# Rotary low-order score product over all 128 rows, and a last projection in four groups of 512 columns

## The chip, the cores and the metric

The kernel runs on one core of one Trainium2 chip, as one launch. The metric is the device time of a run in microseconds (us): 1482.35 us is the median of three runs of the kernel before (1480.5 to 1486.15). The core's engines are named as the profile names them: PE is TensorE (PEld is its loading of weights), DVE is VectorE, ACT is ScalarE, POOL is GpSimd, SP is SyncE, which issues the DMAs.

## What is computed

Two layers of a mixer over 256 context rows and 256 latent rows of width 2048. Each layer normalises and modulates its rows, multiplies by one input projection, and feeds two branches: multi-head latent attention (8 heads, 128 plain and 64 rotary dimensions in a head) and a long convolution of 1024 channels. Both are normalised, gated, joined to 2048 channels and multiplied by one output projection. The second layer computes its queries and its output for the latent rows alone.

The two places that the change touches, in the reference:

```python
s = jnp.einsum("bqhd,bkhd->bhqk", q_nope, k_nope, preferred_element_type=F32)
s = s + jnp.einsum("bqhr,bkr->bhqk", q_rope, k_rope, preferred_element_type=F32)
p = jax.nn.softmax(s * SCALE, axis=-1)
...
y = jnp.concatenate([rmsnorm(o_mla, lp["grp_g_mla"]) * g_m,
                     rmsnorm(y_h, lp["grp_g_hy"]) * g_h], axis=-1)
return rmsnorm(y @ lp["w_out"], lp["post_g"])      # then x + g_x * (...)
```

## The kernel before

**Split products.** Nearly every matrix product takes its fp32 operands as a sum of two parts, a rounded high part (`hi`) and the rest (`lo`), and adds three products: hi·hi, hi·lo, lo·hi (`mm3`). Each of the three is one matmul with its own weight load. Inside a matmul call the first tensor is the one that is loaded (128 columns of it), the second the one that streams through (256 or 512 columns).

**Rotary scores.** In `head_job` the scores of one head and 128 queries are one PSUM tile (`mis` in the profile) made by five matmuls: three of `mm3` over the 128 plain dimensions, and two over the rotary ones. A rotary part has only 64 rows, so `pair_job` stacks its two parts over 128 partitions: for the even head of a pair, rows 0 to 63 hold `hi` and rows 64 to 127 hold `lo`; for the odd head the other way round. The rotary key is written twice over, in both halves, as `kr.hi` and `kr.lo` (`kr_evac` copies it to the second half before the split). One matmul over all 128 rows against `kr.hi` gives (hi + lo)·key-hi. The fifth, line 1191, takes the 64 rows `rr` that hold the query's `hi` against `kr.lo` and gives hi·key-lo.

In layer 0 a head has four such tiles: two against 512 keys and two against 256. In layer 1 it has two, against 512. With 8 heads that is 32 fifth matmuls in layer 0, half of them 512 columns wide and half 256, and 16 in layer 1 of 512 columns.

**The last output projection.** Layer 1's output has 256 rows and 2048 columns over a depth of 2048. `w_items` with `rows=True` makes it in column groups: in one group the gated rows `ys` are loaded (128 of depth by 128 output rows, `m` = 0 or 1), and the weights stream. A group of 256 columns is cut into four items of 512 KB; an item holds four depth tiles (`j`) of 256 columns. So there are 8 groups of 4 items, and each item is 4 x 2 x 3 = 24 matmuls. Each item is loaded by DMA, split into hi and lo on ACT and DVE, and then used. At the end of a group `out_evac` takes the two PSUM tiles (`acc`): ACT squares each and sums the squares into `oss`, DVE multiplies each by the gate. For the last four items, `by_rows` has PE do all of `m` = 0 first and then all of `m` = 1, and `finish` runs for each `m` on its own: sum of squares, `rs` on POOL, four multiply-adds on DVE, four stores.

**What sets the order.** Every operation is issued by a list scheduler (`Net.run`) that keeps an estimated clock of each engine. Its price of a PE operation counts the streamed columns: it doesn't look at the number of rows. Items of the weight stream ("products", rank 10) fill PE between the steps of the attention heads and the convolution. The order that results is fixed at build time.

Of the kernel before, what the change touches and what calls it, by code (L numbers as in the profile page):

```python
# [9 lines left out]
F32 = mybir.dt.float32  # L10
F32R = mybir.dt.float32r
AF = mybir.ActivationFunctionType
ALU = mybir.AluOpType
# [156 lines left out]
class Net:  # L170
# [16 lines left out]

# [1 line left out]
    # Jobs yield operations. A list scheduler issues, of those that could start first by an  # L189
    # estimate of every engine's queue, the one of the lowest rank, so that no queue is held up  # L190
    # by an operation that waits while another one could run.
    def start_of(self, op):
# [120 lines left out]

# [1 line left out]
    def job(self, name, gen, after=(), want=8, rank=5):  # L315
# [109 lines left out]

# [1 line left out]
    def split(self, hi, lo, src):  # L427
# [70 lines left out]

# [1 line left out]
    def setup(self):  # L500
# [67 lines left out]

# [1 line left out]
    def ada_first(self, sec, t0, t1):  # L570
# [121 lines left out]

# [1 line left out]
    def sine(self, n, ps, b, freq):  # L694
# [99 lines left out]

# [1 line left out]
    def load_x(self):  # L796
# [64 lines left out]

# [1 line left out]
    def w_items(self, src, width, xs, evac, need=(), rows=False, parts=False):  # L863
        hold = {}
        out = []
        dup = width == 64
        wid = P if dup else width
        mt = wid // P
        for b in range(4):
            def load(raws, b=b):  # L870
                if dup:
                    yield self.dma(raws[0][:, 512:768], src[b])
                else:
                    yield from self.load(raws[0], src[b])

            def prep(raws, hi, lo):
                if dup:
                    v = raws[0][:, 512:768].rearrange("p (j c) -> p j c", j=4)
                    h = hi[:, 0:512].rearrange("p (j r c) -> p j r c", j=4, r=2)
                    yield from self.split(h[:, :, 0], h[:, :, 1], v)  # L880
                elif isinstance(raws[0], Pair):
                    for k in range(2):
                        r = slice(k * 512, (k + 1) * 512)
                        yield from self.split(hi[:, r], lo[:, r], raws[0].halves[k])
                else:
                    yield from self.split(hi, lo, raws[0])

            def pe(w, b=b, ms=range(mt), js=range(4)):
                if parts or "ps" not in hold:
                    if len(self.acc.free) < mt:  # L890
                        yield lambda: len(self.acc.free) >= mt
                    hold["ps"] = [self.acc.get() for _ in range(mt)]
                for j in js:
                    x = xs(4 * b + j)
                    first, last = ((b == 0 or parts) and j == js[0]), ((b == 3 or parts) and j == js[-1])
                    n = free_size(x.hi)
                    for m in ms:
                        ps = hold["ps"][m]
                        if rows:
                            yield from self.mm3(ps[:, 0:wid], x[:, m * P:(m + 1) * P], w[:, j * wid:(j + 1) * wid],  # L900
                                                first, last)
                        elif dup:
                            both = w.hi[:, j * P:(j + 1) * P]
                            yield self.mm(ps[:, 0:n], both, x.hi, first, False)
                            yield self.mm(ps[:, 0:n], both, x.lo, False, last)
                        else:
                            yield from self.mm3(ps[:, 0:n], w[:, j * wid + m * P:j * wid + (m + 1) * P], x,
                                                first, last)

            def post(b=b, ms=range(mt)):  # L910
                ps = list(hold["ps"])
                for m in ms:
                    if parts and m not in hold:
                        hold[m] = (yield from self.sget())[0]
                        yield self.either(hold[m], ps[m])
                    elif parts:
                        yield self.tt(hold[m], hold[m], ps[m], ALU.add)
                    else:
                        yield from evac(m, ps[m])
                    self.acc.put(ps[m])  # L920
                if parts and b == 3:
                    for m in range(mt):
                        yield from evac(m, hold[m])
                        self.slots.put(hold[m])
            out.append(Item(load, prep, pe, post if b == 3 or parts else None,
                            need=need(b) if callable(need) else (need if b == 0 else ()), halves=not dup))
        return out
# [104 lines left out]

# [1 line left out]
    def raw_evac(self, l, tile0, name, parts, width, c0, n):  # L1034
# [59 lines left out]

# [1 line left out]
    def pair_job(self, l, hp, nq):  # L1096
# [76 lines left out]
    def head_job(self, l, h, nq):  # L1173
# [3 lines left out]
        kk, qq = st["qk"].pop(h)  # L1177
        rr = slice(i * ROPE, (i + 1) * ROPE)
        rq, kr = res["r"][i], st["kr"]
# [3 lines left out]
        for q0, nk in (((nq - L, T),) if nq == L else ((L, T), (0, L))):  # L1183
            pr = []
            pps = []
            for qi in range(2):
                r = slice(q0 + qi * P, q0 + (qi + 1) * P)
                (ps,) = yield from self.pget()
                yield from self.mm3(ps[:, 0:nk], qq[:, r], kk[:, 0:nk], True, False)
                yield self.mm(ps[:, 0:nk], rq[:, r], kr.hi[:, 0:nk], False, False)  # L1190
                yield self.mm(ps[:, 0:nk], rq[rr, r], kr.lo[rr, 0:nk], False, True)
                (p,) = yield from self.sget()
                sm = self.small.tile([P, 4], F32, tag="sm", name="sm")
                yield self.vmax(sm[:, 0:1], ps[:, 0:nk])
                yield self.ts(sm[:, 1:2], sm[:, 0:1], -SCALE, None, ALU.mult)
                yield self.act(p[:, 0:nk], ps[:, 0:nk], AF.Exp, bias=sm[:, 1:2], scale=SCALE, accum_out=sm[:, 2:3])
                self.mis.put(ps)
                yield self.recip(sm[:, 3:4], sm[:, 2:3])
                yield self.either(p[:, 0:nk], p[:, 0:nk], sm[:, 3:4])
                pr.append(p)  # L1200
# [50 lines left out]

# [1 line left out]
    def conv(self, l, ps, ci, nq):  # L1253
# [176 lines left out]

# [1 line left out]
    def z_evac(self, s, g):  # L1432
# [70 lines left out]

# [1 line left out]
    def out_evac(self, g):  # L1505
        st = self.st[1]

        def evac(m, ps):
            if g == 0 and m == 0:
                st["oss"] = self.const.tile([P, 2, 8], F32, name="oss")  # L1510
                st["zo"] = []
                for _ in range(2):
                    st["zo"].append((yield from self.sget(4)))
            j, o = divmod(g * 256, 512)
            junk = (yield from self.sget())[0]
            yield self.act(junk[:, 0:256], ps[:, 0:256], AF.Square, accum_out=st["oss"][:, m, g:g + 1])
            self.slots.put(junk)
            yield self.tt(st["zo"][m][j][:, o:o + 256], ps[:, 0:256], self.gate[j][:, o:o + 256], ALU.mult)
        return evac
# [24 lines left out]

# [1 line left out]
    def layer_items(self, l, nq):  # L1546
# [76 lines left out]
    def build(self):  # L1623
# [52 lines left out]
        for s in (1, 0):  # L1676
            for g in range(8):
                r = slice(s * L, (s + 1) * L)
                need = (lambda b: tuple(f"ys0_{4 * b + j}" for j in range(4))) \
                    if (s, g) == (1, 0) else ()  # L1680
                items += self.w_items(a["p_wout"][0, g], 256, lambda kt, r=r: self.st[0]["ys"][kt][:, r],
                                      self.z_evac(s, g), need)
# [22 lines left out]
        def need_y(b):  # L1705
            return tuple(f"ys1_{4 * b + j}" for j in range(4)) + ("gate",)
        for g in range(8):
            items += self.w_items(a["p_wout"][1, g], 256, lambda kt: self.st[1]["ys"][kt],
                                  self.out_evac(g), need_y if g == 0 else (), rows=True)
# [62 lines left out]
def lay_out(i):  # L1772
# [30 lines left out]
    def tiles(v):  # L1803
        n = v.shape[-1] // 256
        return v.reshape(2, 4, 4, P, n, 256).transpose(0, 4, 1, 3, 2, 5).reshape(2, n, 4, P, 1024)
    o["p_win"] = np.concatenate([tiles(w[:, :, 0:OFF_KR]), tiles(w[:, :, OFF_HY:OFF_GH]),
                                 tiles(w[:, :, OFF_GM:OFF_HY]), tiles(w[:, :, OFF_GH:])], axis=1)
    o["p_wkr"] = w[:, :, OFF_KR:OFF_GM].reshape(2, 4, 4, P, 64).transpose(0, 1, 3, 2, 4).reshape(2, 4, P, 256)
    o["p_wout"] = tiles(i["w_out"])
    uq = i["w_uq"].reshape(2, 4, P, HEADS, HEAD_Q)  # L1810
# [25 lines left out]
```

## Time and profile before

| | before |
|---|---|
| runs | 1480.5, 1482.35, 1486.15 us |
| the profiled execution, first to last instruction | 1483.1 us |
| PE busy | 1457.0 us, 98% |
| DVE busy | 1190.2 us, 80% |
| ACT busy | 692.6 us, 47% |
| DMA queue q1, share of 16 engines | 64.6% |

The profile gives one execution. Its time is its span: no separate time of that execution outside the span is shown. A PE matmul's duration overlaps with that of the next one, so a rate is read from starts: the start of one merged row to the start of the next, divided by the matmuls in the first. By the trace the kernel's stages lie so: up to about 316 us the modulation, the filters and layer 0's first products; 316 to 548 layer 0's attention heads, with weight items between them; 548 to 800 the convolution and the rest of layer 0's input products; 800 to 1158 layer 0's output projection, the step between the layers and layer 1's first products; 1158 to 1278 layer 1's heads; 1278 to 1382.9 the rest of its input products; 1382.9 to 1475.2 the last projection; then the tail.

### The profile page before, as it was taken

The numbers are of one execution on the slowest core, as the hardware profiler recorded it, in microseconds if no ns is written. First come the engines' busy times: TensorE is split into PE (matmuls) and PEld (weight loads), VectorE is DVE, ScalarE is ACT, GpSimd is POOL, SyncE is SP. The second block draws the span as 40 slices with busy tenths as digits, with TensorE's granted clock in tenths as the row PEclk, the third lists the DMA queues.
The fourth block names the chain that finished last, engine by engine and source line by source line (L and its number), as shares of the span: only waits on it lengthen the run. The fifth ranks groups of instructions, "written<-read, shape, count | busy, mean of one in ns | idle before, by whom it ended". The sixth has DMA issues, their size and how long they took to land.

```text
span 1483.1 us, 26318 instructions
## 1 busy us (share of the span) xinstructions
PE 1457.0 (98%) x9700; PEld 1261.2 (85%) x9700; DVE 1190.2 (80%) x2522; ACT 692.6 (47%) x1339; POOL 16.4 (1%) x20
## 2 busy tenths in 40 slices
PE   7999999999999999999999999999999999999997
PEld 5677787778787777877778999999999989999997
DVE  5577999997888878998888988888868878786544
ACT  5421354335354452334334444566646666655542
POOL 0000000000000000000000000000000000000000
PEclk9999999999999999999999999999999999999999
DMA  9997875468466677566858886567728234668441
GB/s 324 356 334 239 286 263 205 159 212 308 151 195 215 223 250 251 170 228 220 299 191 301 296 281 196 167 227 260 245 89 310 90 113 133 234 201 288 164 143 57
DMA packets 165872, 328.92 MB, mean 222 GB/s; under 512 B 18501, under 2 KB 41068, under 8 KB 165744
## 3 DMA queue, kind: packets, MB, share of 16 engines
q1 hardware_dynamic: 165744, 327.25, 64.6%
q8 instruction: 76, 1.25, 0.3%
q14 instruction: 52, 0.43, 0.1%
HBM read 301.99 MB, written 25.18 MB: 221 GB/s over the span
## 4 chain that ended last, share of the span: by engine, by line
PE 88%; DMA 7%; DVE 2%; issue 1%; SPq 1%; ACT 1%; POOL 0%; DVEq 0%; POOLq 0%; ACTq 0%
PE acc L232 68%; PE mis L232 17%; PE mis L235 3%; DMA s<-in_p_ada_first 1%; DMA raw<-in_p_ada_first 1%; DMA s<-in_p_ada_slow 1%; DVE s L250 1%; DMA s<-in_p_win 1%; SPq L309 1%; DMA s<-in_ctx 1%; DVE junk L280 1%; DMA s<-in_p_uv 0%; DMA raw<-in_p_win 0%; DMA s<-in_p_ada_rest 0%; DMA h_d<-s 0%
## 5 line engine op out<-in xcount | busy, mean ns | idle before, releaser
L232 PE MATMUL acc<-s,hi 128*128 128x256 f32 (+1 forms) x2304 | 566.0, 337 | 0.5 <-ACT hi L243 0.4
L232 PE MATMUL acc<-s,s 128*128 128x256 f32 (+1 forms) x3216 | 489.4, 308 | 0.0
L232 PEld LDWEIGHTS acc<-s,s 128*128 128x128 f32 x3216 | 439.2, 191 | 30.5 <-issue 3.7
L232 PEld LDWEIGHTS acc<-s,hi 128*128 128x128 f32 x2304 | 388.4, 191 | 56.2 <-issue 11.5
L250 DVE TENSOR_TENSOR s<-s,s 128x512 fp32r<-128x512 f32 (+5 forms) x575 | 342.2, 623 | 42.3 <-ACT s L245 21.2
L232 PE MATMUL acc<-s,raw 128*128 128x256 f32 (+1 forms) x1104 | 371.1, 336 | 0.3 <-DVE raw L250 0.3
L280 DVE SCALAR_TENSOR_TENSOR junk<-s,s 128x512 bf16<-128x512 f32 x352 | 241.5, 686 | 26.9 <-DMA s<-crow_d 10.5
L232 PE MATMUL mis<-s,s 128*128 128x256 f32 (+2 forms) x1232 | 251.4, 341 | 1.2 <-ACT s L243 0.9
L232 PEld LDWEIGHTS acc<-s,raw 128*128 128x128 f32 x1104 | 210.3, 191 | 23.0 <-issue 2.5
L232 PEld LDWEIGHTS mis<-s,s 128*128 128x128 f32 (+1 forms) x1232 | 190.4, 189 | 43.9 <-issue 13.9
L243 ACT CAST s<-s 128x512 fp32r<-128x512 f32 (+3 forms) x324 | 180.3, 589 | 74.8 <-DVE s L250 28.5
L243 ACT CAST hi<-raw 128x1024 fp32r<-128x1024 f32 (+1 forms) x100 | 97.2, 972 | 121.4 <-PE acc L232 68.7
L250 DVE TENSOR_TENSOR raw<-raw,hi 128x1024 fp32r<-128x1024 f32 x88 | 107.3, 1220 | 19.7 <-ACT hi L243 19.1
L243 ACT CAST hi<-s 128x512 fp32r<-128x512 f32 x124 | 73.4, 618 | 92.9 <-PE acc L232 75.6
L250 DVE TENSOR_TENSOR raw<-s,hi 128x512 fp32r<-128x512 f32 x124 | 83.8, 686 | 34.4 <-ACT hi L243 33.4
L243 ACT COPY s<-mis 128x512 f32<-128x512 f32 (+3 forms) x101 | 48.6, 485 | 116.7 <-PE mis L232 90.5
L250 DVE TENSOR_TENSOR s<-mis,s 128x512 fp32r<-128x512 f32 (+2 forms) x128 | 84.6, 669 | 22.8 <-ACT s L243 17.3
L243 ACT CAST s<-mis 128x512 fp32r<-128x512 f32 (+1 forms) x100 | 56.6, 570 | 89.2 <-PE mis L235 48.3
L245 ACT ACTIVATE s<-acc 128x256 f32<-128x256 f32 (+1 forms) x88 | 37.5, 429 | 96.6 <-PE acc L232 81.2
L235 PE MATMUL mis<-ident,s 128*128 128x128 f32 (+1 forms) x369 | 66.8, 291 | 4.1 <-DMA s<-in_x 1.0
L250 DVE TENSOR_TENSOR s<-raw,s 128x512 fp32r<-128x512 f32 x106 | 69.8, 683 | 0.8 <-ACT s L243 0.7
L243 ACT CAST s<-raw 128x512 fp32r<-128x512 f32 x106 | 61.8, 617 | 9.1 <-DMA raw<-in_p_wout 6.2
(85 smaller groups left out, 916.9 us busy)
## 6 DMA issues: line engine op xcount, KB each, us to landing
s<-in_p_ada_slow SPq DMA_DIRECT2D x208, 256.0 KB, 3.3
raw<-in_p_win SPq DMA_DIRECT2D x99, 512.0 KB, 5.1
s<-in_p_win SPq DMA_DIRECT2D x178, 256.0 KB, 5.3
s<-in_p_wout SPq DMA_DIRECT2D x108, 256.0 KB, 4.9
raw<-in_p_wout SPq DMA_DIRECT2D x42, 512.0 KB, 3.8
s<-in_p_ada_first SPq DMA_DIRECT2D x62, 256.0 KB, 5.8
raw<-in_p_ada_first SPq DMA_DIRECT2D x25, 512.0 KB, 6.1
raw<-in_p_ada_rest SPq DMA_DIRECT2D x20, 512.0 KB, 4.7
```

The lines of the kernel that those rows point to most:

```text
L232: lambda: self.nc.tensor.matmul(out, lhsT, rhs, start=start, stop=stop), 0.2)
L235: return Op("pe", 0.11, [out], [in_], lambda: self.nc.tensor.transpose(out, in_, ident), 0.2)
L243: self.nc.scalar.copy(out, in_)
L245: self.nc.scalar.activation(out, in_, func, **kw)
L250: return Op("dve", fixed + n * rate, [out], ins, lambda: getattr(self.nc.vector, name)(out=out, **kw))
L280: lambda: self.nc.vector.scalar_tensor_tensor(out=junk, in0=a, scalar=1.0, in1=b, op0=ALU.mult, op1=ALU.mult, accum_out=acc))
L309: return Op("sp", n / 360e3, [dst], [src], lambda: self.nc.sync.dma_start(dst, src))
```

## The change

One matmul in five of the rotary scores now runs over all 128 rows, as the one before it does. It then also adds lo·key-lo. The last projection runs over four groups of 512 columns; an item is still 512 KB, but holds two depth tiles of 512 columns, so a group has eight items and an item 2 x 2 x 3 = 12 matmuls. The weights of the last projection are laid out for that on the host and are an input of their own. The evacuation of a group works on 512 columns. The diff, without removed comments:

```diff
@@ w_items
-        mt = wid // P
-        for b in range(4):
+        mt = 2 if rows else wid // P
+        nj = 1024 // width if rows else 4
+        nb = KT // nj
+        for b in range(nb):
...
-            def pe(w, b=b, ms=range(mt), js=range(4)):
+            def pe(w, b=b, ms=range(mt), js=range(nj)):
...
-                    x = xs(4 * b + j)
-                    first, last = ((b == 0 or parts) and j == js[0]), ((b == 3 or parts) and j == js[-1])
+                    x = xs(nj * b + j)
+                    first, last = ((b == 0 or parts) and j == js[0]), ((b == nb - 1 or parts) and j == js[-1])
@@ head_job
-        rr = slice(i * ROPE, (i + 1) * ROPE)
...
-                yield self.mm(ps[:, 0:nk], rq[rr, r], kr.lo[rr, 0:nk], False, True)
+                yield self.mm(ps[:, 0:nk], rq[:, r], kr.lo[:, 0:nk], False, True)
@@ out_evac
-                st["oss"] = self.const.tile([P, 2, 8], F32, name="oss")
+                st["oss"] = self.const.tile([P, 2, 4], F32, name="oss")
...
-            j, o = divmod(g * 256, 512)
-            yield self.act(junk[:, 0:256], ps[:, 0:256], AF.Square, accum_out=st["oss"][:, m, g:g + 1])
+            yield self.act(junk, ps, AF.Square, accum_out=st["oss"][:, m, g:g + 1])
-            yield self.tt(st["zo"][m][j][:, o:o + 256], ps[:, 0:256], self.gate[j][:, o:o + 256], ALU.mult)
+            yield self.tt(st["zo"][m][g], ps, self.gate[g], ALU.mult)
@@ build
-            return tuple(f"ys1_{4 * b + j}" for j in range(4)) + ("gate",)
-        for g in range(8):
-            items += self.w_items(a["p_wout"][1, g], 256, lambda kt: self.st[1]["ys"][kt],
+            return (f"ys1_{2 * b}", f"ys1_{2 * b + 1}", "gate")
+        for g in range(4):
+            items += self.w_items(a["p_wout1"][g], 512, lambda kt: self.st[1]["ys"][kt],
                                   self.out_evac(g), need_y if g == 0 else (), rows=True)
@@ lay_out
-    o["p_wout"] = tiles(i["w_out"])
+    o["p_wout0"] = tiles(i["w_out"][0:1])[0]
+    o["p_wout1"] = i["w_out"][1].reshape(8, 2, P, 4, 512).transpose(3, 0, 2, 1, 4).reshape(4, 8, P, 1024)
```

On every engine the order of instructions is the same up to the last projection; the heads' matmuls stand where they stood (the order names a matmul by its output, so a row does not tell how many rows it multiplies). The first difference on PE is the first item of the last projection. Names there: `acc_181` and `acc_182` are the PSUM tiles of output rows 0 to 127 and 128 to 255, the first name behind the arrow is the streamed weight (hi or lo), the second the loaded `ys`. Before:

```order
L232 MATMUL acc_181_16036<-s_2039_15891,s_1980_15493 128x256
L232 MATMUL acc_181_16036<-s_2041_15893,s_1980_15493 128x256
L232 MATMUL acc_181_16036<-s_2039_15891,s_1980_15493 128x256
L232 MATMUL acc_182_16037<-s_2039_15891,s_1980_15493 128x256
L232 MATMUL acc_182_16037<-s_2041_15893,s_1980_15493 128x256
L232 MATMUL acc_182_16037<-s_2039_15891,s_1980_15493 128x256
L232 MATMUL acc_181_16036<-s_2039_15891,s_1981_15500 128x256
L232 MATMUL acc_181_16036<-s_2041_15893,s_1981_15500 128x256
```

And now:

```order
L232 MATMUL acc_181_16036<-s_2039_15891,s_1980_15493 128x512
L232 MATMUL acc_181_16036<-s_2041_15893,s_1980_15493 128x512
L232 MATMUL acc_181_16036<-s_2039_15891,s_1980_15493 128x512
L232 MATMUL acc_182_16037<-s_2039_15891,s_1980_15493 128x512
L232 MATMUL acc_182_16037<-s_2041_15893,s_1980_15493 128x512
L232 MATMUL acc_182_16037<-s_2039_15891,s_1980_15493 128x512
L232 MATMUL acc_181_16036<-s_2040_15892,s_1981_15500 128x512
L232 MATMUL acc_181_16036<-s_2042_15894,s_1981_15500 128x512
```

The sequence of three by two stays; each matmul is twice as wide, and the next depth tile (`s_1981`) comes with the next half of the weights, so that an item is over after two depth tiles. The other place is the end of DVE's queue: the last multiply by the gate, the sum for `rs`, and the four multiply-adds of output rows 128 to 255. One piece of the difference:

```order
-L250 TENSOR_TENSOR s_2087_16212<-acc_196_17062,s_1988_15544 128x256
+L250 TENSOR_TENSOR s_2101_16254<-acc_188_16616,s_1988_15544 128x512
 L289 TENSOR_REDUCE mf<-oss 128x1
 L250 TENSOR_SCALAR ms<-mf 128x1
-L250 SCALAR_TENSOR_TENSOR s_2084_16209<-s_2084_16209,rf,s_1993_15559 128x512
-L250 SCALAR_TENSOR_TENSOR s_2085_16210<-s_2085_16210,rf,s_1994_15560 128x512
-L250 SCALAR_TENSOR_TENSOR s_2086_16211<-s_2086_16211,rf,s_1995_15561 128x512
```

The same steps follow each other there; only the multiply by the gate, and ACT's square before it, have 512 columns.

## Rows read from the trace of the kernel before

**Rows 1.** The page: busy us, share of the span and instructions of each engine

```profile
PE 1457.0 (98%) x9700; PEld 1261.2 (85%) x9700; DVE 1190.2 (80%) x2522; ACT 692.6 (47%) x1339; POOL 16.4 (1%) x20
```

**Rows 2.** Windows: length, busy PE, PEld, DVE, ACT, POOL (instructions), granted clock, DMA share, GB/s

```profile
316.00:548.00 232.00, 231.66 (x1145) 180.10 (x1144) 194.31 (x485) 112.58 (x215) 0.00 (x0) 1.00 0.66 216
548.00:800.00 252.00, 251.33 (x1163) 198.40 (x1162) 222.46 (x460) 88.35 (x139) 2.77 (x2) 1.00 0.69 237
1158.00:1278.00 120.00, 119.15 (x830) 105.39 (x829) 96.35 (x203) 74.86 (x156) 0.00 (x0) 1.00 0.39 127
1382.90:1475.20 92.30, 92.28 (x769) 92.07 (x768) 46.72 (x84) 38.87 (x93) 0.55 (x1) 1.00 0.33 112
```

**Rows 3.** PE's waits, 174.8 to 1475 us: total, times, longest; first and last of five

```profile
PE mis L232 <- ACT s L243: 0.9, 1, 0.9
...
PE mis L232 <- DVE s L250: 0.2, 1, 0.2
```

**Rows 4.** Groups by form on PE: count, busy us, mean ns

```profile
L232 PE MATMUL mis<-s,s 128*128 128x512 f32 x544 | 145.6, 398 | 0.1
L232 PE MATMUL mis<-s,s 128*128 128x256 f32 x640 | 91.8, 285 | 1.1 <-ACT s L243 0.9 <-DVE s L250 0.2
...
L232 PE MATMUL mis<-s,s 64*128 64x512 f32 x32 | 15.9, 495 | 0.0
...
L232 PE MATMUL mis<-s,s 64*128 64x256 f32 x16 | 6.1, 380 | 0.0
```

**Rows 5.** Timeline of PE, a score tile of 512 keys: start, us, instructions

```profile
322.92 1.50 PE L232 MATMUL mis<-s,s 128*128 128x512 f32 x5
324.35 0.50 PE L232 MATMUL acc<-s,hi 128*128 128x512 f32 x1
324.68 0.39 PE L232 MATMUL acc<-s,raw 128*128 128x512 f32 x1
```

**Rows 6.** Timeline of PE, a score tile of 256 keys

```profile
502.05 0.94 PE L232 MATMUL mis<-s,s 128*128 128x256 f32 x5
502.92 0.50 PE L232 MATMUL acc<-s,hi 128*128 128x512 f32 x1
503.25 0.39 PE L232 MATMUL acc<-s,raw 128*128 128x512 f32 x1
```

**Rows 7.** Timeline of PE, a score tile of layer 1

```profile
1275.82 1.52 PE L232 MATMUL mis<-s,s 128*128 128x512 f32 x5
1277.28 0.62 PE L232 MATMUL acc<-s,s 128*128 128x256 f32 x3
1277.73 0.40 PE L232 MATMUL acc<-s,hi 128*128 128x256 f32 x2
```

**Rows 8.** Timeline of PE, unbroken runs of 512 and of 256 columns

```profile
764.69 8.55 PE L232 MATMUL acc<-s,s 128*128 128x512 f32 x37
1388.62 5.92 PE L232 MATMUL acc<-s,s 128*128 128x256 f32 x48
```

**Rows 9.** Timeline from 1474.5 us: the first steps of the tail

```profile
1475.21 0.38 ACT L245 ACTIVATE s<-acc 128x256 f32<-128x256 f32 x1 [5.28 <-PE acc L232]
1475.72 0.42 DVE L250 TENSOR_TENSOR s<-acc,s 128x256 f32<-128x256 f32 x1 [1.60 <-ACT s L245]
```

**Rows 10.** Groups by form on ACT and DVE: the wider operations

```profile
L245 ACT ACTIVATE s<-acc 128x512 f32<-128x512 f32 x16 | 9.4, 596 | 33.1 <-PE acc L232 33.0
L250 DVE TENSOR_TENSOR s<-mis,s 128x512 f32<-128x512 f32 x28 | 18.7, 686 | 5.2 <-PE mis L235 3.9 <-DMA s<-in_k_decay 1.0
```

**Rows 11.** A window and PE's timeline in it, early in layer 0

```profile
157.30:164.00 6.70, 5.73 (x20) 3.98 (x21) 6.56 (x18) 5.11 (x10) 0.00 (x0) 0.50 1.03 405
...
157.44 0.65 PE L232 MATMUL mis<-s,cs 128*32 128x128 f32 x8 [1.06 <-DMA s<-in_p_ada_first]
...
161.69 0.63 PE L232 MATMUL acc<-s,raw 128*128 128x512 f32 x1
...
162.97 0.63 PE L232 MATMUL acc<-s,raw 128*128 128x512 f32 x1
```

More of the change, by code (lines that the diff above doesn't have):

```diff
@@ L920, in post @@
                     self.acc.put(ps[m])
-                if parts and b == 3:
+                if parts and b == nb - 1:
                     for m in range(mt):
@@ L924, in post @@
                         self.slots.put(hold[m])
-            out.append(Item(load, prep, pe, post if b == 3 or parts else None,
+            out.append(Item(load, prep, pe, post if b == nb - 1 or parts else None,
                             need=need(b) if callable(need) else (need if b == 0 else ()), halves=not dup))
@@ L1680, in build @@
                     if (s, g) == (1, 0) else ()
-                items += self.w_items(a["p_wout"][0, g], 256, lambda kt, r=r: self.st[0]["ys"][kt][:, r],
+                items += self.w_items(a["p_wout0"][g], 256, lambda kt, r=r: self.st[0]["ys"][kt][:, r],
                                       self.z_evac(s, g), need)
@@ L1804, in tiles @@
         n = v.shape[-1] // 256
-        return v.reshape(2, 4, 4, P, n, 256).transpose(0, 4, 1, 3, 2, 5).reshape(2, n, 4, P, 1024)
+        return v.reshape(-1, 4, 4, P, n, 256).transpose(0, 4, 1, 3, 2, 5).reshape(-1, n, 4, P, 1024)
     o["p_win"] = np.concatenate([tiles(w[:, :, 0:OFF_KR]), tiles(w[:, :, OFF_HY:OFF_GH]),
```

## The prediction

> **What bounds the kernel now.** I read the page's busy shares first. PE is busy for 98% of the span, DVE for 80% [rows 1]. A busy share alone does not make PE the bound, so next come the windows by stage: in layer 0's heads PE is busy for 231.66 of 232 us, in layer 1's for 119.15 of 120, in the last projection for 92.28 of 92.3, at the full clock (1.00, the level of 2.4 GHz) in each [rows 2]. Then PE's waits: between 174.8 and 1475 us there are five kinds, once each, from 0.9 down to 0.2 us [rows 3]. So from 174.8 us on, what PE does per matmul is the time, and everything the change saves on PE there is saved for the run, unless something else becomes late. The last view is PE's timeline, for what one matmul takes from start to start. The unbroken runs give it: 37 matmuls of 512 columns last 8.55 us with the last one's own 0.39, so (8.55 - 0.39) / 36 = 0.227 us each; 48 of 256 columns last 5.92, one lasts 0.285, so (5.92 - 0.28) / 47 = 0.120 us each [rows 4, 5, 8].
>
> **The rotary product.** The scores' five matmuls should follow each other like any others. They don't. In a tile of 512 keys the five begin at 322.92 and the next matmul at 324.35: 1.43 us, where five ordinary ones take 5 x 0.227 = 1.13. The matmul after them takes 0.33 to the next start instead of 0.227. Together 0.30 + 0.10 = 0.40 us too many [rows 5]. With 256 keys: 0.87 against 5 x 0.12 = 0.60, and again 0.33 against 0.227: 0.37 us [rows 6]. In layer 1: 1.46 against 1.13, then three of 256 columns in 0.45 against 0.36: 0.42 us [rows 7]. The odd one among the five is the one with 64 rows; its own mean is 495 ns where the form with 128 rows has 398, and 380 against 285 with 256 columns [rows 4]. It also makes its neighbours on both sides late. There are 48 of them (32 and 16 by form [rows 4]), 16 of each of the three kinds: 16 x (0.40 + 0.37 + 0.42) = 19.0 us.
>
> After the change the fifth matmul has the form of the fourth, whose cost the five ordinary ones in the sum already hold. It reads the same two tiles as the fourth does (all 128 rows of the rotary query, and `kr.lo`, split together with `kr.hi`), so it adds no wait. The upper end of the gain is 19.0 us: nothing odd is left. The lower end is the part that surely hangs on the 64 rows, the matmul's own excess: 48 x 0.097 = 4.7 us [rows 4], if the late neighbours had another cause, such as the end of the accumulation. I exclude a loss: the fourth matmul shows the new form. I take 19.0, because the fives with nothing else odd in them show the whole excess three times alike.
>
> By the Trainium skill's "TensorE: Matmul & The Clock Gate" (the table "Why this matters for your kernels") a lone matmul over few rows takes as long as one over 128 rows, which would make this edit worth nothing; rows 4 to 7 disagree. The skill's "TensorEngine Tiling" (Key Properties) says that a change of tiling mode, not of tile, drains the engine, and such a drain would stand once before and once after each 64-row matmul; the late neighbours in rows 5 to 7 agree with that.
>
> **The last projection.** Removed: 8 groups x 4 items x 24 = 768 matmuls of 256 columns, 768 x 0.120 = 92.2 us, which is the window's 92.3 [rows 2, 8]. Added: 4 x 8 x 12 = 384 of 512 columns, 384 x 0.227 = 87.0 us (with the unrounded 8.16 / 36). Gain 5.1 us. No row shows weights streamed 512 wide; but at 256 columns it makes no difference which operand streams: the last two matmuls of rows 7 load weights and take 0.40 - 0.28 = 0.12 us, as the projection's do [rows 7, 8]. The ends are 0 (512 columns cost twice 256) and 5.1; I take 5.1.
>
> By the skill's "TensorE: Matmul & The Clock Gate" (Part 1, on the gap of 56 ns) a warm matmul costs its columns at 2.4 GHz plus a fixed 2.5 ns. An estimate by that page is 384 x 2.5 ns = 1.0 us for this edit, and the sum would be 4.1 us higher; rows 8 show a fixed part of 2 x 0.120 - 0.227 = 0.013 us instead.
>
> Beside it: an item now lasts 12 x 0.227 = 2.72 us, not 2.88, with the same 512 KB, the same split. DVE is busy for 46.72 and ACT for 38.87 of 92.3 us there and the DMA engines for 0.33 [rows 2], so all three stay hidden; were that cover gone, PE would fall to their pace, which by these shares is at half of its own. The evacuation of the first three groups lies beside the next group. The need for `ys` is looser: two tiles per item, and the sixteenth only in the eighth item.
>
> **The tail.** The last group's evacuation is on the path, and it is wider. ACT's square takes 0.38 us with 256 columns [rows 9] and 0.596 with 512 [rows 10]: 0.22. DVE's multiply starts only behind it: 0.42 [rows 9] against 0.686 [rows 10]: 0.27. The last matmul itself lasts 0.398 - 0.285 = 0.11 us longer [rows 4]. Cost 0.6 us; nothing hides it. The rest of the tail (the sum, POOL, four multiply-adds, stores) stays.
>
> **Sum.** 1483.1 - 19.0 - 5.1 + 0.6 = 1459.6 us against the profiled span of 1483.1. That span is 0.75 us over the median of the runs, 1482.35, so against the runs it is 1458.85. PE has 0.34 us idle in layer 0's heads and 0.85 in layer 1's [rows 2]; with PE's steps shorter there and the other engines' unchanged, I allow as much again, 1.2 us. Forecast: 1460 us.
>
> **Rivals.**
>
> *DVE becomes the bound in layer 0.* DVE is busy for 194.31 of 232 us in the heads and 222.46 of 252 in the stage behind them [rows 2]. Of the 19.0 us, 16 x (0.40 + 0.37) = 12.3 fall into the first of these. For it: 194.31 of 219.7 us is 88%, the share that the second already has, and an order fixed at build time makes PE stand still whenever one operand is late. Against it: the second stage runs at 88% with PE busy for 251.33 of 252. If the waits take back half of the 12.3 the time is 1466; all of it, 1472. I give it 12%.
>
> *The 64 rows are not the cause* and the excess is that of a tile's last product, or of the step to another PSUM tile. Then the first edit brings 0 to 4.7 us and the time is 1474 to 1479. Against it: the other products end tiles too, and the runs in rows 8 pass many ends of tiles without a pause. 5%. The edit would then not do what it says.
>
> *512 columns cost twice 256.* The 5.1 us don't come: 1465. Against it rows 8. 3%.
>
> *Slower.* PE's faster steps in layer 0's heads meet operands that aren't there, as at 157 us, where PE had waited 1.06 us for a DMA and the clock then stood at 0.50, the level of 1.2 GHz [rows 11]. Three matmuls of 512 columns took 162.97 - 161.69 = 1.28 us there, 0.427 each, so 0.2 us more than at the full clock. To undo 22.4 us of gain and go 7.4 us (0.5%) beyond, 29.8 us must be lost, 149 such matmuls, or 149 x 0.427 = 64 us at the lower level: nine stretches of the 6.7 us of rows 11. From there on it decides, the time is 1490 or more. For it: the heads are the place with the tightest order. Against it: 1300 us without such a wait [rows 3]. 2%.
>
> **How the numbers follow.** The forecast has 78%; its own range is 1457 to 1464. The first rival takes the range up to 1468; that leaves out the rest of it, the second rival and the slower case, and a little below. Range 1456 to 1468. Less than 0.5% (7.4 us) can't be told from no change: faster means below 1475. Faster 0.94: the forecast, the first and third rivals, and a part of the second. Same 0.04, slower 0.02.
>
> **What will show it.** In the profile after: no form with 64 rows in `mis<-s,s`; five score matmuls of 512 keys from start to next start in 1.13 us, and 0.227 for the one after; layer 0's heads 12 us shorter, layer 1's 7; the last projection in 87 us with 512-column matmuls 0.227 apart; from the last matmul's start to the end 0.6 us more. Waits of PE on DVE of several us between 304 and 790 would mean the first rival; a start-to-start excess still at the fifth matmul the second; 0.24 us per matmul in the projection the third; a granted clock under 1.00 after 175 us the last. The forecast is wrong if the time is above 1468.

## The result and the profile after

The changed kernel takes 1464.13 us (median of four runs, 1457.93 to 1468.44) where the kernel before takes 1481.42 beside it: a ratio of 0.9884, 95% interval 0.9851 to 0.9917. Three more comparisons gave 0.9885 (0.9869 to 0.9901), 0.9883 (0.9859 to 0.9906) and 0.9884 (0.9863 to 0.9905). So it is faster by 17 us. The forecast was 1460 us, 22.4 less than the 1482.35 it started from, with a range of 1456 to 1468. The result lies in that range, but 0.1 us above the forecast's own one (1457 to 1464).

The profiled execution after the change has a span of 1456.2 us. The page's first part, answering [rows 1]:

```profile
PE 1428.0 (98%) x9316; PEld 1240.0 (85%) x9316; DVE 1188.4 (82%) x2514; ACT 692.0 (48%) x1323; POOL 16.4 (1%) x20
```

PE lost 29 us of busy time and 384 matmuls, and is still busy for 98%. No engine took its place. The groups by form (count, busy us, mean ns) answer [rows 4]:

```profile
L232 PE MATMUL mis<-s,s 128*128 128x512 f32 x576 | 151.2, 396 | 0.0
L232 PE MATMUL mis<-s,s 128*128 128x256 f32 x656 | 93.3, 284 | 0.9 <-ACT s L243 0.9
```

The 32 and 16 matmuls of 64 rows are now 32 and 16 more of 128 rows, and there is no other form under this name. PE's timeline (start, us, instructions) of three score tiles, with 512 keys, with 256, and in layer 1, answers [rows 5], [rows 6] and [rows 7]:

```profile
317.67 1.30 PE L232 MATMUL mis<-s,s 128*128 128x512 f32 x5
318.80 0.39 PE L232 MATMUL acc<-s,hi 128*128 128x512 f32 x1
319.02 0.39 PE L232 MATMUL acc<-s,raw 128*128 128x512 f32 x1
...
489.44 0.76 PE L232 MATMUL mis<-s,s 128*128 128x256 f32 x5
490.03 0.39 PE L232 MATMUL acc<-s,hi 128*128 128x512 f32 x1
490.26 0.40 PE L232 MATMUL acc<-s,raw 128*128 128x512 f32 x1
...
1253.23 1.32 PE L232 MATMUL mis<-s,s 128*128 128x512 f32 x5
1254.39 0.52 PE L232 MATMUL acc<-s,s 128*128 128x256 f32 x3
1254.74 0.40 PE L232 MATMUL acc<-s,hi 128*128 128x256 f32 x2
```

Five matmuls of 512 columns take 1.13 us to the next start, where it was 1.43, and the one behind them 0.22, where it was 0.33. With 256 keys 0.59 (0.87) and 0.23 (0.33); in layer 1 1.16 (1.46) and 0.35 for three (0.45). The excess of 0.37 to 0.42 us is gone, on both sides of the fifth matmul.

The last projection and the tail, on the same timeline, answer [rows 8] and [rows 9]:

```profile
1365.39 5.60 PE L232 MATMUL acc<-s,s 128*128 128x512 f32 x24
...
1447.19 0.60 ACT L245 ACTIVATE s<-acc 128x512 f32<-128x512 f32 x1 [4.75 <-PE acc L232]
1447.68 0.19 ACT L245 ACTIVATION_READ_ACCUMULATOR s<-acc 128x1 f32 x1
1447.91 0.69 DVE L250 TENSOR_TENSOR s<-acc,s 128x512 f32<-128x512 f32 x1 [1.02 <-ACT s L245]
```

(5.60 - 0.39) / 23 = 0.227 us per matmul, with the weights streaming 512 wide. Against [rows 9], the square takes 0.22 us more and the multiply 0.27, as summed.

Windows of the same stages (columns as in [rows 2]; the bounds are those of the same matmuls as there, found by counting PE's records, which are the same work in the same order up to the projection):

```profile
311.80:531.50 219.70, 218.58 (x1144) 179.27 (x1143) 193.50 (x486) 112.11 (x215) 0.00 (x0) 1.00 0.67 227
531.50:783.40 251.90, 251.32 (x1162) 198.51 (x1161) 222.83 (x461) 88.81 (x139) 2.77 (x2) 1.00 0.71 238
1141.30:1255.10 113.80, 112.88 (x829) 106.34 (x828) 95.63 (x202) 74.77 (x156) 0.00 (x0) 1.00 0.40 132
1359.90:1446.80 86.90, 86.90 (x386) 71.92 (x384) 45.51 (x76) 37.63 (x77) 0.55 (x1) 1.00 0.34 114
```

One trace is one execution. The experiments gave more of both kernels; the table has the same stages, cut at the same matmuls, in us. "Start" is what lies before 174.8 us in the first trace of before, "between" the three stretches that neither edit touches (174.8 to 316, 800 to 1158 and 1278 to 1382.9 us in that trace), the tail runs from the last matmul's start.

| trace | start | between | heads 0 | convolution | heads 1 | projection | tail | span |
|---|---|---|---|---|---|---|---|---|
| before, first | 174.8 | 604.0 | 232.0 | 252.0 | 120.0 | 92.0 | 8.2 | 1483.1 |
| before, second | 173.2 | 604.0 | 231.2 | 252.9 | 119.1 | 92.0 | 8.2 | 1480.7 |
| after, first | 170.2 | 604.2 | 219.8 | 251.9 | 113.9 | 86.8 | 9.4 | 1456.2 |
| after, second | 173.5 | 604.0 | 220.9 | 253.6 | 113.0 | 86.8 | 9.4 | 1461.2 |
| after, third | 174.8 | 604.5 | 222.7 | 253.0 | 112.7 | 86.8 | 9.4 | 1463.9 |
| after, fourth | 174.8 | 604.0 | 222.7 | 253.3 | 112.6 | 86.8 | 9.4 | 1463.7 |

### The profile page after: what moved, and what is told of

It reads as the page before. It is cut to its first block, busy times and chain, and to the rows that moved or that the text cites. A ratio compares the mean times of both kernels' runs of the same rounds, so it can differ in the third digit from the quotient of the medians.

```text
span 1456.2 us, 25519 instructions
## 1 busy us (share of the span) xinstructions
PE 1428.0 (98%) x9316; PEld 1240.0 (85%) x9316; DVE 1188.4 (82%) x2514; ACT 692.0 (48%) x1323; POOL 16.4 (1%) x20
## 4 chain that ended last, share of the span: by engine, by line
PE 87%; DMA 8%; DVE 2%; issue 1%; SPq 1%; ACT 1%; DVEq 0%; POOLq 0%; POOL 0%; ACTq 0%
PE acc L232 68%; PE mis L232 17%; PE mis L235 3%; DMA s<-in_p_ada_first 2%; DMA raw<-in_p_ada_first 1%; DMA raw<-in_p_win 1%; DVE s L250 1%; DMA s<-in_p_win 1%; SPq L309 1%; DMA s<-in_ctx 1%; DMA s<-xt_d 1%; DVE junk L280 0%; DMA s<-in_p_uv 0%; DMA s<-crow_d 0%; DVE raw L250 0%
## 5 line engine op out<-in xcount | busy, mean ns | idle before, releaser
L232 PEld LDWEIGHTS acc<-s,s 128*128 128x128 f32 x2976 | 425.8, 191 | 39.1 <-issue 2.7
L232 PE MATMUL mis<-s,s 128*128 128x256 f32 (+1 forms) x1232 | 239.6, 337 | 0.9 <-ACT s L243 0.9
L232 PEld LDWEIGHTS mis<-s,s 128*128 128x128 f32 x1232 | 189.6, 189 | 30.0 <-ACT s L243 2.4
L235 PEld LDWEIGHTS mis<-ident,s 128*128 128x128 f32 (+1 forms) x369 | 49.1, 155 | 20.5 <-ACT s L243 3.0
```

The costliest lines, as they stand in the source:

```text
L232: lambda: self.nc.tensor.matmul(out, lhsT, rhs, start=start, stop=stop), 0.2)
L235: return Op("pe", 0.11, [out], [in_], lambda: self.nc.tensor.transpose(out, in_, ident), 0.2)
```

## The experiments

All were timed against the kernel before, five rounds each; three more runs of the changed kernel are among them. Times are medians.

**The first edit alone** (order of all engines as before).

```diff
-                yield self.mm(ps[:, 0:nk], rq[rr, r], kr.lo[rr, 0:nk], False, True)
+                yield self.mm(ps[:, 0:nk], rq[:, r], kr.lo[:, 0:nk], False, True)
```

> The kernel before with the fifth score matmul alone over 128 rows; the order of all engines is that of before. If 64 rows cost 0.37 to 0.42 us a time: 17.8 to 19 us less than before, ratio 0.987 to 0.988, and 1158 us later layer 1's heads 6 us shorter. If DVE had become the bound, half of layer 0's part or less: 12 us less, 0.992. If the 64 rows aren't the cause: 0 to 4.7 us less.

Measured: 1465.12 us, ratio 0.9906 (0.9889 to 0.9922), 15.0 us less than before's 1480.14. In its trace the heads take 221.5 and 113.1 us: the edit's stages are those of the changed kernel. The windows of both (columns as in [rows 2]):

```profile
311.70:533.20 221.50, 219.47 (x1145) 179.44 (x1143) 193.77 (x484) 111.98 (x214) 0.00 (x0) 1.00 0.68 224
1143.80:1257.00 113.20, 113.03 (x830) 106.48 (x829) 95.78 (x202) 74.81 (x156) 0.00 (x0) 1.00 0.40 132
```

The size lies between the first and the second expectation, and neither ratio lies in the interval.

**Two matmuls of 64 rows, side by side.** Lo times key-hi is left out.

```diff
-                yield self.mm(ps[:, 0:nk], rq[:, r], kr.hi[:, 0:nk], False, False)
+                yield self.mm(ps[:, 0:nk], rq[rr, r], kr.hi[rr, 0:nk], False, False)
                 yield self.mm(ps[:, 0:nk], rq[rr, r], kr.lo[rr, 0:nk], False, True)
```

> The kernel before with the fourth score matmul too on the 64 rows that the fifth has (the product lo times key-hi is left out); the order of all engines is that of before. Theory 1, the cost is that of going over to 64 rows and back, once for both since they stand side by side: the same time as before (within 2 us), and in a tile the excess 0.37 to 0.42 us as before. Theory 2, each matmul of 64 rows costs its 0.4 us: 48 x 0.4 = 19 us more. Theory 3, the end of a tile is the cost: the same time.

Measured: 1482.63 us, 1.0020 (1.0009 to 1.0031): 2.5 us more than before, where theory 2 wanted 19 and theory 1 at most 2. In four of the 48 tiles the fixed order has other matmuls between the two (at 340, 446, 1234 and 1258 us of its trace). There the second is as slow as the first, and four more goings-over at 0.4 us are 1.6 of the 2.5 us. This fits theory 1, though its text had all 48 side by side.

**The same two, with one matmul of 128 rows between them.**

```diff
-                yield from self.mm3(ps[:, 0:nk], qq[:, r], kk[:, 0:nk], True, False)
-                yield self.mm(ps[:, 0:nk], rq[:, r], kr.hi[:, 0:nk], False, False)
+                yield self.mm(ps[:, 0:nk], qq.hi[:, r], kk.hi[:, 0:nk], True, False)
+                yield self.mm(ps[:, 0:nk], qq.hi[:, r], kk.lo[:, 0:nk], False, False)
+                yield self.mm(ps[:, 0:nk], rq[rr, r], kr.hi[rr, 0:nk], False, False)
+                yield self.mm(ps[:, 0:nk], qq.lo[:, r], kk.hi[:, 0:nk], False, False)
                 yield self.mm(ps[:, 0:nk], rq[rr, r], kr.lo[rr, 0:nk], False, True)
```

> The same five matmuls as in the kernel with two of 64 rows side by side (lo times key-hi left out again), but the first of the two stands one place earlier, with a matmul of 128 rows between them. Theory 1, going over to 64 rows and back costs: twice per tile, so 48 x 0.4 = 19 us more than side by side and than before, ratio to before 1.013, and 0.8 us excess in a tile. Theory 2, each matmul of 64 rows: 19 us more than before here too, but the same as side by side. Theory 3, the end of a tile: the same as before.

Measured: 1503.06 us, 1.0156 (1.0141 to 1.0172): 20.4 us more than side by side, for the same matmuls in another order. With this edit the scheduler also moved other work, from 452 us on, so not all of the 20.4 us need be the tiles'. PE's timeline of one tile of each, side by side first:

```profile
321.83 1.50 PE L232 MATMUL mis<-s,s 128*128 128x512 f32 x5
323.26 0.50 PE L232 MATMUL acc<-s,hi 128*128 128x512 f32 x1
323.59 0.40 PE L232 MATMUL acc<-s,raw 128*128 128x512 f32 x1
```

```profile
323.85 1.90 PE L232 MATMUL mis<-s,s 128*128 128x512 f32 x5
325.67 0.50 PE L232 MATMUL acc<-s,hi 128*128 128x512 f32 x1
326.01 0.39 PE L232 MATMUL acc<-s,raw 128*128 128x512 f32 x1
```

Two side by side: 1.43 us to the next start and 0.33 behind, exactly what one of them costs [rows 5]. Apart: 1.82 and 0.34, so 0.39 to 0.40 more in the tile itself. The groups by form say the same, side by side first:

```profile
L232 PE MATMUL mis<-s,s 64*128 64x512 f32 x64 | 24.1, 448 | 0.0
```

```profile
L232 PE MATMUL mis<-s,s 64*128 64x512 f32 x64 | 31.8, 497 | 0.0
```

448 is about the mean of one slow matmul (497) and one ordinary (398). So the price is for going over to 64 rows and back, about 0.4 us a time, not for a matmul of 64 rows, nor for the end of a tile. That is the Trainium skill's rule in "TensorEngine Tiling (Array Packing)" (Key Properties: changing the mode, not just the tile, drains the engine), and the trace agrees as far as the mode goes; it gives no figure, and here it is 0.4 us. No run here changes the tile alone, and what PE does in the 0.4 us isn't seen.

**The second edit alone** (the fifth matmul on 64 rows, the rest as changed).

> The last projection alone in four groups of 512 columns, the fifth score matmul on 64 rows as before. By rows: 5.1 us less in the projection (384 matmuls 0.227 us apart, 87.0 us), 0.6 to 1.2 us more in the tail, so 3.9 to 4.5 us less, ratio 0.997. If 512 columns cost twice 256: 0.6 to 1.2 us more. In the profile the stages up to the projection are those of before within 1 us each, but for the first 175 us, which scatter by 5.

Measured: 1480.39 us, 0.9991 (0.9978 to 1.0004): not shown to be faster by its times. Its trace has the projection in 86.8 us and the tail in 9.4, both as expected; its windows of heads 0 and of the projection:

```profile
317.50:548.50 231.00, 231.00 (x1145) 180.30 (x1145) 195.78 (x489) 113.14 (x216) 0.00 (x0) 1.00 0.66 217
...
1382.40:1469.30 86.90, 86.90 (x386) 71.93 (x384) 45.50 (x76) 37.63 (x77) 0.55 (x1) 1.00 0.34 114
```

So 4.0 us are gained where the edit acts, and the runs show 0.9: the expected ratio of 0.997 lies outside the interval, a miss. Its start took 175.5 us in the trace, the longest of all. Behind the start, its trace is 5.0 and 4.2 us shorter than the two of before.

**The kernel before, and the changed one, again.**

> The kernel before against itself: ratio 1, and a second trace of it. If the first 175 us scatter from run to run and the rest doesn't: every stage behind 175 us as in the first trace within 1 us, and the first 175 us anywhere from 170 to 175, longer where the granted clock was at 1.2 GHz for longer. If stages behind 175 us scatter too, the 548 to 800 us stage shows it (252 to 253.5 us so far).

Measured: 0.9996 (0.9982 to 1.0009). The start took 173.2 us, and every stage behind it lies within 1 us of the first trace, as expected, though not by much (0.7, 0.9 and 0.9 us in the heads and the convolution): a difference of 1 us in one stage of one trace is no finding.

> The changed kernel once more, with more runs. By the stages of the first profile after the change (layer 0's heads 11.7 us shorter, layer 1's 6.1, the projection 5.1, the tail 1.2 longer) its median should be 21.7 us under the kernel before: a ratio of 0.985, with what lies before 175 us the same on the mean. If the first four runs (17.3 us less, ratio 0.988) are the truth and not scatter, some stage gives 4 us back in runs that weren't profiled.

Measured: 1463.55 us.

> The changed kernel a third time, for a third trace and more runs. If scatter of the first 175 us made the measured gain (16.6 to 17.3 us) smaller than the stages' sum (20.6 to 22.3 us): a gain nearer 20 us here. If a stage behind 175 us gives back what the heads save: the same 16.6 us, and 253 us or more in the stage of the convolution.

Measured: 1463.81 us. The 17 us are no scatter of the runs. Neither expectation fits whole: the convolution's stage is within half a microsecond on the mean (table above), and the gain is not nearer 20. A fourth comparison, beside the two kernels of the next experiment, gave 1464.11 us where 1463.8 was expected, and the table's fourth trace, in the stages as expected.

**Where the inputs lie in memory.** The change makes two input arrays of one. Two kernels, each with the order of its base: the changed one with a single array, and the one before with two. The host side of the second:

```diff
-    o["p_wout"] = tiles(i["w_out"])
+    o["p_wout0"], o["p_wout1"] = tiles(i["w_out"])
```

> The changed kernel with the weights of both output projections in one input array again (the second half in the new layout); the order of all engines is that of the changed kernel. If two arrays in place of one put the inputs at other places in memory and so make the first 175 us some 3 us longer: 1460 to 1461 us, ratio to before 0.986, against 0.9884 of the changed kernel. If the shortfall (17 us measured, 20 by the stages of the traces) is anything else: 0.9884 again, 1463.8 us.

> The kernel before with its output weights in two input arrays, nothing else changed; the order of all engines is that of before. If where the inputs lie is the cause: 3 us slower than before, ratio 1.002, by the first 175 us. If not: ratio 1 within 0.001.

Measured: 1464.42 us, 0.9879 (0.9858 to 0.9899), and 1481.87 us, 1.0003 (0.9992 to 1.0014). The arrays are not the cause: the first interval alone reaches down to the 0.986 of that case, but the second leaves no room for 1.002.

**Two attempts at a faster version**, both on the changed kernel. First, the modulation's items two by two:

```diff
-            while k < len(side) and k < (i + 1) * len(side) / len(main):
+            while k < len(side) and k < (i + 1) * len(side) // (2 * len(main)) * 2:
```

> The changed kernel with the 16 items of the modulation that lie among layer 0's products (matmuls of 32 output rows, in groups of eight records) put two by two instead of one by one. In the traces of before and after, such a group makes PE late by 0.09 us before it and 0.11 behind it, as the 64-row matmul did. If going over to that form and back costs, and not the group: half of the goings-over are gone, 8 x 0.3 = 2.4 us less than the changed kernel (0.2%), between 200 and 790 us. If each group has its own cost: the same. If the items, which each need two loads, come too late in pairs: slower by the waits.

Measured: 1474.31 us, 0.9955 (0.9939 to 0.9971), 10 us slower than the changed kernel. The scheduler put other matmuls between some of the groups again: PE goes over to this form (512 columns wide) 14 times instead of 21, not half as often. And PE waited: behind the start it is idle for 14.9 us, where it is for 3.5 to 5.7 in the four traces of the changed kernel. The timeline and the window at one of the waits:

```profile
496.71 0.86 PE L232 MATMUL mis<-s,s 128*128 128x256 f32 x5 [2.00 <-DVE s L250]
497.50 2.16 PE L232 MATMUL mis<-raw,cs 128*32 128x512 f32 x8
```

```profile
497.00:500.50 3.50, 3.50 (x15) 1.56 (x15) 3.31 (x8) 2.28 (x5) 0.00 (x0) 0.57 1.08 400
```

After a wait of 2.00 us the granted clock is 0.57 on the mean of 3.5 us, so at the lower level (1.2 GHz) for most of them, and the group of eight takes 2.16 us. This is the mechanism of the slower rival; the changed kernel's heads don't show it (clock 1.00).

Second, steps offered later to the scheduler: `EARLY = 0.0` for `0.5`.

> The changed kernel with the scheduler's EARLY at 0 instead of 0.5: a job's next step is offered for the order only when its operands are ready by the scheduler's estimate, not 0.5 us before. In the traces of the changed kernel PE waits 1.5 to 3.3 us in layer 0's heads (0 to 0.5 in those of before). If these waits come of steps that stand a little too early in the order: they fall under 1 us, layer 0's heads take 219.5 to 221 us, and the run is 1 to 2 us faster than the changed kernel. If DVE's or ACT's pace is what PE waits for: the waits move to other places and the time stays. If the later steps leave queues with nothing to do, it is slower.

Measured: 1468.3 us, 0.9905 (0.9883 to 0.9927). The waits moved to other places and the run is not faster: by the medians it is slower, though the interval reaches down to the changed kernel's 0.9884. Neither attempt is a gain.

## Why the prediction was right, and where its sum was off

**The bound.** PE sets the time after the change as before: it is busy for 98% of the span, and what its matmuls saved came out in the time but for new waits, a longer tail and 3 us that stay open, which the points below follow. That step held.

**The rotary term, 19.0 us.** The mechanism held, and was shown by order alone (side by side against apart). The price per tile held too, and new waits took back some of it in layer 0. Layer 1's heads went from 119.1 to 120.0 us to 112.6 to 113.9: 6.5 less by the means, 6.7 expected. Layer 0's went from about 231.6 (mean of the two in the table) to 221.5 (mean of four): 10.1, where 12.3 was expected; the convolution's stage behind them is half a microsecond longer (252.5 to 253.0, means). PE's busy time in layer 0's heads tells price and waits apart: 231.6 and 230.8 us in the two traces of before, 218.6, 219.0, 219.9 and 219.4 in the four after, so 12.0 less on the mean. Nearly all of what is missing from 12.3 is therefore PE's waits, 0.4 us there before and 2.3 after on the mean. In the fourth trace after the change, 312 to 540 us (total, times, longest):

```profile
PE mis L232 <- DVE s L250: 1.7, 2, 0.9
PE mis L235 <- ACT s L245: 1.6, 1, 1.6
```

Before, the five kinds of wait of the whole rest of the run were 0.9 us and less [rows 3]. So the first rival, the operands that come too late for a faster PE, came true for about 2 us of 12.3, not for half; 1.2 us had been allowed. With the convolution and layer 1's heads the new waits are 2.1 us on the mean, so the sum was 0.9 short there. DVE's pace was not the bound: its busy time is as before and its share 87% in the window of that trace:

```profile
316.20:538.90 222.70, 219.37 (x1144) 179.32 (x1143) 193.27 (x485) 112.53 (x214) 0.00 (x0) 1.00 0.68 224
```

What was late were single steps, DVE's and ACT's.

**The projection, 5.1 us.** From 92.0 to 86.8, measured between the first and the last matmul's start: 5.2. Weights that stream 512 wide cost what rows streaming 512 wide do. An estimate by the Trainium skill's fixed 2.5 ns a matmul ("TensorE: Matmul & The Clock Gate", Part 1) gave 1.0 us; the trace disagrees, as [rows 8] did. PEld, the loading of weights, is busy for 92.07 of 92.30 us in the projection before [rows 2] and for 71.92 of 86.90 now. Whether the loads set the pace at 256 columns, and so raise the fixed part, wasn't tried.

**The tail, 0.6 us.** This term was mis-sized: the sum held that the steps behind the multiply stay as they are. Up to the first of the last four multiply-adds the tail is 0.59 us longer, as summed; the whole tail is 1.2 longer in every trace of the changed kernel (0.62 and 0.85 in those of the two attempts at a faster version, with the same projection). The rest lies behind the last store, in its landing and in the program's end, and why those take longer wasn't tried.

**Sum.** The stages give -10.1 + 0.5 - 6.5 - 5.2 + 1.2 = -20.1 us, where the forecast had -22.4 with its allowance. The times give -17. That the range held owes something to its upper end, which was widened for the first rival: only a part of the 5 us by which the forecast was too low is that rival's. Also, the base was read wrongly. The result lists times and spans, and a time is 1.8 us more than its span (1457.93 and 1456.2). By that the first trace of before, 1483.1, came from a run of about 1484.9, 2.5 us over the median and not 0.75: a long one, in part by its start of 174.8 us. This made no difference to the forecast, which took the change from the median.

**What stays open** are the 3 us between the stages and the times. They are a difference between the executions that have a trace and the others. The two traces of before are of runs 2.5 and 1.3 us over the medians of their kernel; the four after the change are of runs from 6.2 under to 1.9 over, 0.9 under on the mean: 1.9 + 0.9 = 2.8 us. In which stage the other runs spend them isn't shown. The start is in no edit's reach and scatters by 5 us from trace to trace; over all comparisons but that of the last attempt the granted clock's mean was 0.9957 for the changed kernel (21 runs, the single-array one among them) and 0.9963 for the one before (63 runs). By an estimate from these means, that is 2 x 0.0006 x 1470 = 1.8 us more at half the clock, so 0.9 us lost. The shortfall is larger with the second edit: alone it misses 3.1 us of the 4.0 by its stages, at a mean clock of 0.9952 (12 runs) against 0.9963 beside it, 1.6 us by the same estimate; the first edit alone misses 1.3 us of 16.3. Why the second kernel runs longer at the lower clock isn't known. Where the inputs lie is excluded. Only one execution of each kernel in a comparison has a trace, so whether the untraced runs lose the remainder in the start or in waits in layer 0 can't be told.

## What to carry to other kernels

Look at the starts of the matmuls around an odd form, not at the mean of the odd one: its group's mean showed 4.7 us of excess of 19. By the starts in the trace of before, the odd one holds 0.20 us, the matmul before it 0.09 and the one behind it 0.11. A few short matmuls over fewer rows in a stream of full ones can cost more than the arithmetic that they save; keep them side by side, or make them full with rows that are there anyway. And where an order is fixed at build time by prices, a stage that gets faster returns some of the gain as waits, so subtract something for it, here a sixth of the heads' part in layer 0 (1.9 of 12.0 us).

## What was not expected of the hardware

A matmul of 64 rows next to another of 64 rows costs no more than one of 128: in the 29 tiles of 512 keys where nothing stands between the two, the second lasts 388 to 394 ns, where the form with 128 rows has 398 on the mean. And the clock's fall in the paired kernel came after a single wait of 2.00 us: of the 17 us up to 497 PE was busy for 15.00, at a granted clock of 1.00, the last four of them partly in groups of the form 128*32. It made the eight records take 2.16 us; the same group in the changed kernel:

```profile
487.41 1.06 PE L232 MATMUL mis<-raw,cs 128*32 128x512 f32 x8
```
